# One level of Strassen's algorithm for the large products of a decoder layer in split fp32

## The chip, the cores and the metric

The kernel runs on one core of a Trainium2 chip. The metric is the device time of one execution in microseconds (us). In the profile PE is TensorE (PEld its weight loads), DVE is VectorE, ACT is ScalarE, POOL is GpSimd and SP the engine that issues the transfers; PEclk is the granted TensorE clock as a share of full speed.

## The reference

One decoder layer for 1,024 tokens of 1,024 channels, all in fp32:

```python
def _swiglu(xn, w_gate, w_up, w_down):
    return (jax.nn.silu(xn @ w_gate) * (xn @ w_up)) @ w_down
...
    u = jax.nn.gelu(z[..., :i1])
    v = jax.nn.gelu(z[..., i1:i2])
    c = z[..., i2:i3]
    ga = z[..., i3:i4]
    gb = z[..., i4:]
    a = _spatial_gating(u, v, sgu_norm_g, sgu_w, sgu_b)
    b = _pool_mixer(c, pool_w, pool_scale)
    y = jax.nn.sigmoid(ga) * (a @ w_out_a) + jax.nn.sigmoid(gb) * (b @ w_out_b)
    return y @ w_o
...
        f = _swiglu(_rmsnorm(h, ffn1_pre_g[i]), ffn1_w_gate[i], ffn1_w_up[i], ffn1_w_down[i])
        h = h + 0.5 * _rmsnorm(f, ffn1_post_g[i])
        m = _token_mixer(_rmsnorm(h, mix_pre_g[i]), w_in[i], sgu_norm_g[i], sgu_w[i], sgu_b[i],
                         pool_w[i], pool_scale[i], w_out_a[i], w_out_b[i], w_o[i])
        h = h + _rmsnorm(m, mix_post_g[i])
        f = _swiglu(_rmsnorm(h, ffn2_pre_g[i]), ffn2_w_gate[i], ffn2_w_up[i], ffn2_w_down[i])
        h = h + 0.5 * _rmsnorm(f, ffn2_post_g[i])
        gate = jax.nn.sigmoid(_rmsnorm(h, ple_pre_g[i]) @ ple_w_gate[i])
        e = p[i] @ ple_w_proj[i]
        h = h + _rmsnorm(gate * e, ple_post_g[i])
```

Here `z = xn @ w_in` has 5 x 1,024 columns; the feed-forward layers are 2,816 wide. The spatial gating multiplies each chunk of 128 positions by four masked 128 x 128 matrices; the pool mixer takes trailing means and one 256 x 256 product per group of channels. There are two feed-forward layers, before and after the mixer, with weights of their own.

## The kernel before

Every fp32 product is made of three TensorE products of fp32r parts: an operand is split into hi (a cast on ScalarE) and lo (the operand less hi, on VectorE), and `mm3` adds lo x hi, hi x lo and hi x hi into one PSUM bank of 128 x 512 (lines 134 to 136). The activations stand transposed in SBUF as two halves of 512 tokens, hi and lo, for a whole stage.

The weights come through one ring for the whole program, the class `Weights`: it lists all weight tiles (512 KB each, 128 x 1,024 elements) in the order of their use, loads two ahead, splits them (cast on line 67, subtraction on line 68) and holds four split tiles. A tile is split as soon as a place in the ring is free, whatever stage it belongs to.

A feed-forward layer (`ffn`) goes through 11 groups of 256 hidden channels. For a group it makes gate and up products (`gate_up`: 512 tokens a bank, Silu on ScalarE, multiplication and split), and with a lag of one group the down product of these channels for all eight token tiles (`down`), which VectorE adds into SBUF (line 383). The hidden activations never leave SBUF. With the last group's down product each token tile is closed: post-norm, residual, pre-norm of the next stage (lines 420, 421, 157; the squares on ScalarE, line 147, the reciprocal root on GpSimd, lines 141 and 142), and, LAG = 3 tiles later, its transposes (line 180) and the first products of the next stage (`follow`) are put between the down products.

The mixer then makes v and u by tokens, c with the pooled channels, the gates, the branches a and b and the output projection, each with the weights of the ring; the layer ends with the second feed-forward layer and the gate with the embedding p.

The order of each engine's instructions comes from a scheduler of the framework, which works from the order in the code and the dependences. Each engine runs its instructions in order. All transfers are issued by SP, in order as well.

## Time and profile before

| | |
|---|---|
| time, median of 3 runs | 2355.18 us (2353.83 to 2357.21) |
| span of the profiled execution (its time from the first to the last instruction) | 2353.6 us |
| mean granted TensorE clock | 0.998 |
| matmuls of 128x512 / of 128x256 / of 128x128 and transposes | 9,984 / 96 / the rest of 10,420 |
| bytes moved, mean rate | 179.60 MB, 76 GB/s |
| weight splits of 128x1024: cast, subtraction | 202 x 1,054 ns, 202 x 1,222 ns |
| additions of the down products into SBUF | 320 x 686 ns |

A group's row reads: line, engine, operation, output <- inputs, shape, count, busy time and the mean of one. Matmuls overlap, so that the mean of one (389 ns) is longer than the time from one to the next. A timeline row reads: start, duration, engine, line, operation, and in brackets the idle time before it and what ended it.

### The profile page before, as it was taken

The page shows a single profiled execution, that of the slowest core. Times are in us where ns is not written, and L with a number is a line of the kernel's source. Part 1 is how long each engine was busy: PE and PEld are TensorE (multiplying, and loading weights), DVE is VectorE, ACT ScalarE, POOL GpSimd, SP SyncE. Part 2 cuts the span into 40 slices and gives each one's busy share as a digit, 9 for nine tenths or more (in the row PEclk, how much of TensorE's full clock was granted, in tenths as well). Part 3 has the DMA queues.
Part 4 walks back from the last instruction along what each step waited for, and adds up shares of the span by engine and source line. Part 5 has one row for each costly group of instructions (what it writes and reads, how often), then busy time and mean ns, then how long its engine had stood idle before and what let it go on. Part 6 is the DMA issues. An engine that isn't in the chain of part 4 may idle for free.

```text
span 2353.6 us, 24731 instructions
## 1 busy us (share of the span) xinstructions
PE 2324.4 (99%) x10420; PEld 1925.2 (82%) x10420; DVE 928.5 (39%) x1164; ACT 556.6 (24%) x837; POOL 111.2 (5%) x200
## 2 busy tenths in 40 slices
PE   8999999999999999999999999999999999999998
PEld 6888888888887888888888888788888888888877
DVE  5233333333336652353112253633333333333574
ACT  6211111111112423232221121421111111111252
POOL 1000000000001220000000000200000000000051
PEclk9999999999999999999999999999999999999999
DMA  8111111111112321124233341521111111111323
GB/s 277 53 39 52 54 36 54 54 46 45 54 58 90 126 63 36 49 89 136 90 97 95 123 142 41 176 92 54 44 46 54 54 45 45 54 45 45 98 95 103
DMA packets 179695, 179.60 MB, mean 76 GB/s; under 512 B 7936, under 2 KB 141568, under 8 KB 179584
## 3 DMA queue, kind: packets, MB, share of 16 engines
q1 hardware_dynamic: 179584, 178.03, 23.8%
q8 instruction: 81, 1.33, 0.2%
q14 instruction: 30, 0.25, 0.0%
HBM read 148.64 MB, written 29.36 MB: 76 GB/s over the span
## 4 chain that ended last, share of the span: by engine, by line
PE 64%; DVE 1%; POOL 1%; ACT 1%; issue 0%; DMA 0%; POOLq 0%; DVEq 0%; ACTq 0%
PE ps L134 21%; PE ps L135 21%; PE ps L136 21%; PE ps L180 1%; ACT wk L147 0%; DVE X L421 0%; POOL sc L142 0%; POOL sc L141 0%; DVE wk L157 0%; DMA raw<-in_ffn_w_gate_dram 0%; POOL X L668 0%; POOL part L153 0%; DVE wlo L68 0%; DVE X L420 0%; DVE X L130 0%
## 5 line engine op out<-in xcount | busy, mean ns | idle before, releaser
L135 PE MATMUL ps<-X,whi 128*128 128x512 f32 x2080 | 807.4, 389 | 0.0
L136 PE MATMUL ps<-X,whi 128*128 128x512 f32 x2080 | 807.3, 389 | 0.0
L134 PE MATMUL ps<-X,wlo 128*128 128x512 f32 x2080 | 802.1, 390 | 0.2 <-ACT X L129 0.2
L134 PE MATMUL ps<-whi,X 128*128 128x512 f32 x1184 | 462.1, 392 | 5.0 <-DVE X L130 5.0
L135 PE MATMUL ps<-wlo,X 128*128 128x512 f32 x1184 | 461.7, 390 | 0.0
L136 PE MATMUL ps<-whi,X 128*128 128x512 f32 x1184 | 461.6, 390 | 0.0
L134 PEld LDWEIGHTS ps<-X,wlo 128*128 128x128 f32 x2080 | 390.3, 188 | 81.3 <-ACT X L129 0.7
L136 PEld LDWEIGHTS ps<-X,whi 128*128 128x128 f32 x2080 | 390.5, 188 | 81.1
L135 PEld LDWEIGHTS ps<-X,whi 128*128 128x128 f32 x2080 | 390.5, 188 | 80.5
L67 ACT CAST whi<-raw 128x1024 fp32r<-128x1024 f32 (+1 forms) x206 | 213.4, 1046 | 915.1 <-PE ps L134 518.6
L68 DVE TENSOR_TENSOR wlo<-raw,whi 128x1024 fp32r<-128x1024 f32 (+1 forms) x206 | 247.9, 1212 | 410.8 <-ACT whi L67 386.5
L383 DVE TENSOR_TENSOR X<-X,ps 128x512 f32<-128x512 f32 x320 | 218.7, 686 | 160.9 <-PE ps L136 160.9
L134 PEld LDWEIGHTS ps<-whi,X 128*128 128x128 f32 x1184 | 223.0, 188 | 51.3 <-DVE X L130 5.9
L136 PEld LDWEIGHTS ps<-whi,X 128*128 128x128 f32 x1184 | 223.0, 188 | 46.5
L135 PEld LDWEIGHTS ps<-wlo,X 128*128 128x128 f32 x1184 | 223.1, 188 | 45.3
L362 DVE TENSOR_TENSOR hf<-hf,ps 128x512 f32<-128x512 f32 x88 | 60.5, 688 | 500.4 <-PE ps L136 492.6
L129 ACT CAST X<-hf 128x512 fp32r<-128x512 f32 x88 | 54.6, 621 | 241.3 <-DVE hf L362 241.3
L361 ACT ACTIVATE hf<-ps 128x512 f32<-128x512 f32 x88 | 52.4, 595 | 169.1 <-PE ps L136 169.1
L130 DVE TENSOR_TENSOR X<-hf,X 128x512 fp32r<-128x512 f32 x88 | 60.6, 688 | 28.8 <-ACT X L129 28.8
L130 DVE TENSOR_TENSOR X<-ps,X 128x512 fp32r<-128x512 f32 x85 | 55.1, 683 | 19.2 <-ACT X L129 18.8
L141 POOL TENSOR_SCALAR sc<-sc 128x1 f32<-128x1 f32 x48 | 19.2, 400 | 828.6 <-ACT wk L147 827.5
L147 ACT ACTIVATE wk<-X 128x1024 f32<-128x1024 f32 (+1 forms) x48 | 47.4, 989 | 41.4 <-DVE X L421 32.4
(95 smaller groups left out, 875.0 us busy)
## 6 DMA issues: line engine op xcount, KB each, us to landing
raw<-in_ffn_w_gate_dram SPq DMA_DIRECT2D x44, 512.0 KB, 3.7
raw<-in_ffn_w_up_dram SPq DMA_DIRECT2D x44, 512.0 KB, 3.7
raw<-in_ffn_w_down_dram SPq DMA_DIRECT2D x44, 512.0 KB, 3.7
raw<-in_w_in_dram SPq DMA_DIRECT2D x40, 512.0 KB, 3.7
ld<-h SPq DMA_DIRECT2D x16, 512.0 KB, 3.6
X<-in_x_dram SPq DMA_DIRECT2D x8, 512.0 KB, 10.3
ld<-in_x_dram SPq DMA_DIRECT2D x8, 512.0 KB, 4.3
e<-hf SPq DMA_DIRECT2D x16, 256.0 KB, 4.0
```

What stands on the lines that cost most here:

```text
L67: nc.scalar.copy(hi, raw)
L68: nc.vector.tensor_tensor(lo, raw, hi.bitcast(F32), op=ALU.subtract)
L129: nc.scalar.copy(hi, src)
L130: nc.vector.tensor_tensor(lo, src, hi.bitcast(F32), op=ALU.subtract)
L134: nc.tensor.matmul(ps, wl[1], wr[0], start=first, stop=False)
L135: nc.tensor.matmul(ps, wl[0], wr[1], start=False, stop=False)
L136: nc.tensor.matmul(ps, wl[0], wr[0], start=False, stop=last)
L147: nc.scalar.activation(junk, src, AF.Square, accum_out=ss)
L180: nc.tensor.transpose(ps[:, j * P:(j + 1) * P], src[:, c * P:(c + 1) * P], ident)
L361: nc.scalar.activation(s, pg, AF.Silu)
L362: nc.vector.tensor_tensor(s, s, pu, op=ALU.mult)
L383: nc.vector.tensor_tensor(f[:, cols], f[:, cols], ps, op=ALU.add)
```

## The change

Every large product is cut into 2 x 2 blocks of its three matrices, and seven block products, of sums of blocks, stand in place of eight (Winograd's form: 7 products; 4 sums of the left blocks, 4 of the right, 7 of the results). The blocks of a product's left side are 512 x 512 for the mixer's products. The three-part split is as before, of each of the seven operands. The class `Weights` and the function `ffn` are gone; each stage has pools of its own, which are opened when the stage begins and closed when it ends.

The order of the seven products and the PSUM banks: two banks X and Y for each output block's set of four; a product with `True` begins its bank, the others add to it, so that part of the result sums is made in PSUM.

```diff
+ORDER = (("p1", "X", True), ("p2", "Y", True), ("p5", "Y", True), ("p6", "X", False),
+         ("p3", "Y", False), ("p7", "X", False), ("p4", "X", False))
...
+        def sums(self, k, cols, a11, a12, a21, a22, tmp):
+            s1, s2, s4 = tmp(), tmp(), tmp()
+            nc.vector.tensor_tensor(s1, a22, a21, op=ALU.subtract)
+            self.put(2, k, cols, s1)
+            self.put(6, k, cols, a22)
+            nc.vector.scalar_tensor_tensor(s2, a11, -1.0, s1, op0=ALU.mult, op1=ALU.subtract)
+            self.put(3, k, cols, s2)
+            nc.vector.tensor_tensor(a21, a11, a21, op=ALU.subtract)
+            self.put(5, k, cols, a21)
+            nc.vector.scalar_tensor_tensor(s4, a12, -1.0, s2, op0=ALU.mult, op1=ALU.subtract)
+            self.put(4, k, cols, s4)
...
+        def read(self, name):
+            x, y, at = self.b.get("X"), self.b.get("Y"), self.place
+            if name == "p1":
+                nc.scalar.copy(at("11"), x)
+            elif name == "p2":
+                nc.vector.tensor_tensor(at("11"), at("11"), y, op=ALU.add)
+                self.final("11", at("11"))
+            elif name == "p5":
+                nc.scalar.activation(at("22"), y, AF.Copy, scale=-1.0)
+            elif name == "p6":
+                nc.scalar.activation(at("12"), x, AF.Copy, scale=-1.0)
+            elif name == "p3":
+                nc.vector.tensor_tensor(at("12"), at("12"), y, op=ALU.subtract)
+                self.final("12", at("12"))
+            elif name == "p7":
+                nc.vector.tensor_tensor(at("22"), at("22"), x, op=ALU.subtract)
+                self.final("22", at("22"))
+            else:
+                self.final("21", x)
```

`put` splits one operand into hi and lo. The left operands of a stage are seven tiles of a pool of seven. `feed` makes them out of a token tile by eight transposes: for the upper four tiles it keeps the blocks and makes operands 0 and 1, for the lower four it makes the sums above.

`columns` makes products with weights as the stationary side, for a group of 256 weight columns of each half at a time: `prepare(g)` loads the four blocks, makes 4 additions and 7 splits of 128 x 1,024, and is called for the next group after this group's third product. It serves the hidden stage (11 groups), u and c, the gates (4 groups each) and the branches (2 groups each). `rows` does the same with tokens as the stationary side, for v, the output projection and the last gate.

A feed-forward layer is two stages now. The first writes the seven sums of the hidden activations and four of the down weights' sums into DRAM, per group; the second (`ffn_down`) loads both operands of each of the seven products again, splits them and accumulates over the 11 blocks in PSUM:

```diff
+            def after(c):
+                g = hid.pop(c)
...
+                keep(0, g["11"])
+                keep(1, g["12"])
+                keep(6, g["22"])
+                s1, s2, s3, s4 = (new() for _ in range(4))
+                nc.vector.tensor_tensor(s1, g["22"], g["21"], op=ALU.subtract)
+                keep(2, s1)
...
+                down_sums(c)
...
+            l = s_d[s][i][:, c * HT:(c + n) * HT].rearrange("p (k f) -> p k f", k=n)
+            for j, d in enumerate((l, right(i, c, n))):
+                ld = q.tile([P, 2, HT], F32, name="land", tag="land", bufs=4)[:, 0:n]
+                nc.sync.dma_start(ld, d)
+                split(o[:, j, 0, 0:n], o[:, j, 1, 0:n], ld)
...
+        def final(t, half, part):
+            ft = tiles[t]
+            if t >= 4 and half == 0:
+                nc.scalar.copy(ft[:, half * HT:(half + 1) * HT], part)
+            if half != (1 if t < 4 else 0):
+                return
+            hp = load(q, src(t), lds)
+            xn = work(q, wks)
+            r = rsqrt(squares(ft, xn), factor / D, factor * EPS)
+            nc.vector.tensor_tensor(ft, ft, g_post, op=ALU.mult)
+            nc.vector.scalar_tensor_tensor(ft, ft, r, hp, op0=ALU.mult, op1=ALU.add)
+            nc.sync.dma_start(dst[t], ft)
+            pre_norm(ft, g_pre, xn)
+            left.feed(xn, t)
```

`final` is the closing of a token tile (`closing`): the upper four tiles are complete with p3, the lower four with p4, the last product. There is no lag: a tile's transposes follow its norms at once. The large products done so are gate, up and down, the five of `w_in`, both branches, the output projection and the last gate; the pooled channels' products and the projection of p are as they were. The spatial products have v as the stationary side now and 128 columns each, with the bias in an addition on VectorE; the results u, c, a and y go through DRAM between the stages.

**TensorE at a stage end.** In the first feed-forward layer's down stage, before, the transposes of a token tile (line 180, `wk` is the normed tile) stand between down products whose operands have been there for long (`whi`, `wlo`: activations and weights split before):

```order
L134 MATMUL ps_4818<-whi_4540,X_4301 128x512
L135 MATMUL ps_4818<-wlo_4541,X_4301 128x512
L136 MATMUL ps_4818<-whi_4540,X_4301 128x512
L180 MATMUL ps_4826<-ident_135,wk_4721 128x128 x4
L180 MATMUL ps_4833<-ident_135,wk_4721 128x128 x4
L134 MATMUL ps_4859<-whi_4534,X_4301 128x512
```

Now the first token tile's transposes (line 167) stand right between the end of p3 (`X_4549`, which completes this tile) and the start of p7 (`X_4720`):

```order
L86 MATMUL ps_4003<-X_4549 128x512
L87 MATMUL ps_4003<-X_4549 128x512
L88 MATMUL ps_4003<-X_4549 128x512
L167 MATMUL ps_4590<-ident_117,wk_4573 128x128 [waits DVE_49]
L167 MATMUL ps_4590<-ident_117,wk_4573 128x128 x3
L167 MATMUL ps_4595<-ident_117,wk_4573 128x128 x4
L86 MATMUL ps_3612<-X_4720 128x512 [waits DVE_49,Activation_49]
```

The transposes moved from three tiles after the end of their tile's products to the place directly behind them.

**VectorE at the same stage's end.** Before, the splits of the next weights (line 68) stand among the closings of the last tiles (lines 420, 421 and 157; line 130 splits transposed tiles):

```order
L157 SCALAR_TENSOR_TENSOR wk_4990<-X_1144,sc_5003,g_4697 128x1024
L68 TENSOR_TENSOR wlo_5101<-raw_4687,whi_5100 128x1024
L420 TENSOR_TENSOR X_1144<-X_1144,g_4695 128x1024
L68 TENSOR_TENSOR wlo_5107<-raw_4693,whi_5106 128x1024
L130 TENSOR_TENSOR X_4702<-ps_5138,X_4701 128x4x128
L421 SCALAR_TENSOR_TENSOR X_1144<-X_1144,sc_5069,ld_5007 128x1024
```

Now the last token tile's sums (lines 149 to 156) and operand splits (line 82, `X`) come first, and the first split of the next stage's weights (`wr_5321`, for v) stands behind all of them:

```order
L149 TENSOR_TENSOR hf_5280<-ps_5273,hf_5278 128x512
L152 SCALAR_TENSOR_TENSOR hf_5281<-f_4713,hf_5280 128x512
L154 TENSOR_TENSOR hf_5278<-f_4713,hf_5278 128x512
L82 TENSOR_TENSOR X_5105<-hf_5280,X_5105 128x4x128
L156 SCALAR_TENSOR_TENSOR hf_5282<-f_4713,hf_5281 128x512
L82 TENSOR_TENSOR X_5108<-ps_5273,X_5108 128x4x128
L82 TENSOR_TENSOR X_5112<-hf_5281,X_5112 128x4x128
L82 TENSOR_TENSOR X_5116<-hf_5278,X_5116 128x4x128
L82 TENSOR_TENSOR X_5120<-hf_5282,X_5120 128x4x128
L82 TENSOR_TENSOR wr_5321<-land_5317,wr_5321 128x1024
L82 TENSOR_TENSOR wr_5324<-land_5319,wr_5324 128x1024
```

The weights' splits moved from among the closings to behind the last of them.

**SP between the two stages of a feed-forward layer.** There was no such place before. Now the loads of the down stage (line 441, `land`) stand behind the stores of the last group's sums (lines 403 and 397; `so` are sums made by VectorE):

```order
L403 DMA ffn1_s4_128<-so_3572 128x512
L397 DMA ffn1_t20_138<-so_3584 128x512
L397 DMA ffn1_t30_139<-so_3587 128x512
L397 DMA ffn1_t50_140<-so_3590 128x512
L397 DMA ffn1_t60_141<-so_3593 128x512
L113 DMA g_3608<-in_ffn1_post_g_dram 128x1024
L113 DMA g_3610<-in_mix_pre_g_dram 128x1024
L441 DMA land_3617<-ffn1_s0_124 128x1024
L441 DMA land_3621<-in_ffn1_w_down_dram 128x2x512
L441 DMA land_3650<-ffn1_s0_124 128x1024
```

What is new in this queue are all the stores and the two gains ahead of the first load.

More of the change, by code (lines that the diff above doesn't have):

```diff
@@ L1 @@
-from contextlib import ExitStack
+from contextlib import ExitStack, contextmanager
 import concourse.bass as bass
@@ L343, in layer_kernel @@
[L343 to L373 removed]
+    ws_t = const.tile([P, 2, SGU_G, P], FR, name="ws_t")
@@ new lines, in down_stage, with new @@
+    def down_stage(s, src, dst, next_g):
+        with stage(f"{s}b") as q:
+            def new():
+                return q.tile([P, D], F32, name="f", tag="f", bufs=9)
+            f = [new() for _ in range(NT)]
+            g_post, g_pre = gain(q, a[f"{s}_post_g"][0]), gain(q, next_g)
+            nxt = Seven(q, new)
+            ffn_down(s, q, closing(q, f, 4.0, src, dst, g_post, g_pre, nxt))
+        return nxt
+    ffn_hidden("ffn1", left)
+    left = down_stage("ffn1", lambda t: x[t * P:(t + 1) * P, :], h1_d, a["mix_pre_g"][0])
@@ new lines, in layer_kernel, with new @@
+    with stage("o") as q:
+        def new():
+            return q.tile([P, D], F32, name="m", tag="m", bufs=9)
+        m = [new() for _ in range(NT)]
+        g_post, g_pre = gain(q, a["mix_post_g"][0]), gain(q, a["ffn2_pre_g"][0])
+        left = Seven(q, new)
+        rows(q, ysum, a["w_o"][0], closing(q, m, 1.0, lambda t: h1_d[t], h2_d, g_post, g_pre, left, 1, 2), lands=6, wts=2)
+    ffn_hidden("ffn2", left)
+    h3_d = scratch("h3_", NT)
+    left = down_stage("ffn2", lambda t: h2_d[t], h3_d, a["ple_pre_g"][0])
```

1020 lines of the change are left out of this document (515 added, 505 removed).

## The prediction, as put on record before the change was run

> **What bounds the kernel now.** I read the page first (totals, then the chain that ended last), then the groups with shapes kept apart, then busy time by window, then the timeline of single engines at a stage end.
>
> ```profile
> span 2353.6 us, 24731 instructions
> PE 2324.4 (99%) x10420; PEld 1925.2 (82%) x10420; DVE 928.5 (39%) x1164; ACT 556.6 (24%) x837; POOL 111.2 (5%) x200
> PE 64%; DVE 1%; POOL 1%; ACT 1%; issue 0%; DMA 0%; POOLq 0%; DVEq 0%; ACTq 0%
> ```
>
> TensorE is busy for 99% of the span and is the only engine with a real share of the chain (what the chain line lacks to 100% is its short pieces). VectorE has 61% idle, ScalarE 76%. So each matmul taken out is worth its full step, as long as TensorE stays the bound. The step is not the mean duration, since matmuls overlap; it comes from a window that holds nothing but feed-forward work:
>
> ```profile
> core 0: us, PE busy (x) PEld busy (x) DVE busy (x) ACT busy (x) POOL busy (x), PEclk, DMA share, GB/s
> 0.00:60.00 60.00, 49.96 (x232) 40.90 (x233) 31.19 (x36) 36.38 (x62) 7.86 (x39) 0.97 0.80 272
> 1600.00:2100.00 500.00, 500.00 (x2208) 414.15 (x2207) 180.33 (x234) 82.69 (x106) 0.00 (x0) 1.00 0.16 49
> ```
>
> 500.00 / 2208 = **0.2265 us** for a 128x512 matmul. The span is 1.6 us below the median of the runs, 2355.18; I sum in the span and add 1.6 at the end.
>
> **What goes.** The order of the instructions holds 8,760 matmuls of 512 columns after the change, where there were 9,984: 1,224 x 0.2265 = 277 us less. It is not a full eighth, since the pooled channels and the small projection of p stay as they are. The 96 spatial matmuls of 256 columns become 192 of 128, and 276 transposes stay (272 before): 468 short ones. A group of eight transposes shows their step:
>
> ```profile
> 765.78 1.03 PE L180 MATMUL ps<-ident,wk 128*128 128x128 f32 x8
> 766.57 0.48 PE L134 MATMUL ps<-whi,X 128*128 128x512 f32 x1
> ```
>
> 0.79 / 8 is 0.10; with the gap to the next matmul 0.11. No row has an fp32r matmul of 128 columns; 0.06 (a quarter of the 512 step) and 0.23 (the whole of it) bound it, 12 to 43 us for the 192; I take the transpose's 0.11. TensorE's work is then 8,760 x 0.2265 + 468 x 0.11 = 1984 + 51 = **2035 us**. If nothing else made it wait beyond what it does today, the span would be about 2,085 (today's waits are 2353.6 less 9,984 x 0.2265, less 42 of short matmuls: 50 us).
>
> **What comes.** Every operand is a sum that has to be made and split. In the order, VectorE's subtractions and additions of 128x1024 go from 240 to 616, those of 128x512 between SBUF tiles from 164 to 506, its PSUM additions fall from 533 to 363; ScalarE's casts of 128x1024 go from 222 to 430; the loads and stores on SP go from 398 to 1,102, their bytes from 180 to about 367 MB. Steps, from start to start at a stage end:
>
> ```profile
> 767.73 1.28 DVE L157 SCALAR_TENSOR_TENSOR wk<-X,sc,g 128x1024 f32<-128x1024 f32 x1 [2.19 <-POOL sc L142]
> 768.93 1.22 DVE L420 TENSOR_TENSOR X<-X,g 128x1024 f32<-128x1024 f32 x1
> 770.06 0.69 DVE L458 BATCH_NORM_STATS2 st<-X 128x6 f32<-128x512 f32 x1
> ...
> 771.85 0.68 DVE L383 TENSOR_TENSOR X<-X,ps 128x512 f32<-128x512 f32 x1
> 772.45 1.28 DVE L421 SCALAR_TENSOR_TENSOR X<-X,sc,ld 128x1024 f32<-128x1024 f32 x1
> ```
>
> ```profile
> 789.53 1.06 ACT L147 ACTIVATE wk<-X 128x1024 f32<-128x1024 f32 x1 [0.15 <-DVE X L421]
> 790.50 0.18 ACT L147 ACTIVATION_READ_ACCUMULATOR wk<-X 128x1 f32 x1
> 790.59 1.03 ACT L67 CAST whi<-raw 128x1024 fp32r<-128x1024 f32 x1
> 791.52 1.06 ACT L147 ACTIVATE wk<-X 128x1024 f32<-128x1024 f32 x1
> ```
>
> VectorE: 1.13 us for 1024 columns of two tiles, 1.20 with a scalar, 0.60 for 512. ScalarE: 0.93 for a cast, 1.06 for squares. VectorE's sum over the program is then about 1,500 us, ScalarE's 980: both below TensorE's 2,035. So the average says that all is hidden. By stage it is not, and the queues are in order, so I go through the stages (TensorE / VectorE in us, from counts and steps): prologue 31 / 42; hidden of each feed-forward 419 / 258; down 216 / 150; v 97 / 77; u and c 152 / 74; gates 174 / 105; **branches a and b 152 / 174**; **output projection 83 / 87**; last gate 76 / 62. Two stages are VectorE's. Inside hidden, u and c, and the first four products of down, each wait of TensorE is for work that VectorE's order has several us earlier, so I cost those at nothing; their cover is VectorE's idle 40%, and 419 us for the 66 MB of hidden's loads and stores (158 GB/s, less than the 272 of the first row above). Were the cover gone, each microsecond per group would be 22 in the 22 groups.
>
> **Where TensorE waits.** These are the terms; each is a chain that stands between two matmuls in the order.
>
> - *Start.* 14 us until inputs have landed and gone through the first norm, then the prologue's 42 us of VectorE, all ahead of the first weight's split, and some 5 us for hand-offs: 61 where TensorE has 31 to do. **+30** (21 to 41).
> - *Hidden to down, twice.* The first loads stand on SP behind the last group's stores, which wait for VectorE's sums. Nine steps of 0.60, two issues, a landing, two casts, a subtraction:
>
> ```profile
> raw<-in_ffn_w_down_dram SPq DMA_DIRECT2D x44, 512.0 KB, 3.7
> X<-in_x_dram SPq DMA_DIRECT2D x8, 512.0 KB, 10.3
> ```
>
> ```profile
> 783.13 0.33 SPq L423 DMA_DIRECT2D h<-X  x1
> 783.50 0.42 SPq L166 DMA_DIRECT2D ld<-in_x_dram  x1
> ```
>
> 5.4 + 0.8 + 3.7 + 2 x 0.93 + 1.13 + hand-offs of 1 = 14. (The 10.3 is a landing in the burst at the start, for later.) What follows is slow as well:
>
> ```profile
> 769.16 0.39 PE L136 MATMUL ps<-whi,X 128*128 128x512 f32 x1
> 771.39 0.50 PE L134 MATMUL ps<-X 128*128 128x512 f32 x1 [1.84 <-DVE X L130]
> ...
> 773.09 0.63 PE L136 MATMUL ps<-X 128*128 128x512 f32 x1
> 773.51 0.63 PE L134 MATMUL ps<-X 128*128 128x512 f32 x1
> 773.94 0.63 PE L135 MATMUL ps<-X 128*128 128x512 f32 x1
> ```
>
> ```profile
> 770.00:780.00 10.00, 8.61 (x35) 7.05 (x36) 7.23 (x11) 4.09 (x9) 2.19 (x5) 0.83 0.32 106
> ```
>
> After 1.84 us of idleness the granted clock of that window is 0.83, and matmuls come every 0.43 us for about 3 us: 1.6 to 2 us lost behind each long wait. [...] So 14 + 2, twice: **+32** (26 to 40).
> - *Inside down, twice.* The first token tile's eight transposes stand ahead of the seventh factor's matmuls. They wait for its closing: addition 0.6, squares 1.06, multiply 1.13 with POOL beside it, an addition of the next tile 0.6, 1.20, squares 1.06, POOL, 1.20; and then ScalarE's two copies and two casts of the transposed tile (0.5 each) stand ahead of p7's own two casts of 0.93. POOL's pair is one of two lengths:
>
> ```profile
> 766.86 0.19 POOL L141 TENSOR_SCALAR sc<-sc 128x1 f32<-128x1 f32 x1 [2.72 <-ACT wk L147]
> 767.14 0.55 POOL L142 TENSOR_TENSOR sc<-sc,nhalf 128x1 f32<-128x1 f32 x1
> 767.90 1.16 POOL L141 TENSOR_SCALAR sc<-sc 128x1 f32<-128x1 f32 x1 [0.21 <-ACT wk L147]
> 769.14 1.41 POOL L142 TENSOR_TENSOR sc<-sc,nhalf 128x1 f32<-128x1 f32 x1
> ```
>
> 0.83 or 2.65 us. With the short one and hand-offs of 1 that is 8.7 to the transposes, of which TensorE works 2 on the other tiles; then 3.9 of ScalarE's. 10 or 11, and 2 for the clock: **+24** for both stages (12 to 36).
> - *Down to the next stage, twice.* p4 ends all four lower token tiles; each has 1.13 + 1.20 + 1.20 of norms and 4 sums and 5 subtractions of 512, 9 us, and all stand on VectorE ahead of the next weights' split. From the end of the first tile's last matmul: 10 us to its transposes, 31 of queue, 1.2 of split, 2 of gaps; less 6 of matmuls and 3 of transposes. 35 + 2, twice: **+74** (64 to 90). Before, the lag of three tiles hid this.
> - *v to u and c* **+22** (18 to 30): VectorE runs late by 7 at the end of v, then store, load, split. *To the gates* **+11** (8 to 16). *Pooled channels*, four groups, each with a split behind the next group's: **+17** (8 to 26).
> - *Branches and output projection.* VectorE starts 6.5 us late behind stores and loads, has 181 us to the last of the sums, and the output projection's first weights another 10: 198 against TensorE's 152, and 4 for the clock: **+50** (38 to 75).
> - *Output projection to the second feed-forward.* VectorE has 67 us left when p3 ends, 50 into the 83: 117 less 83, hand-offs 6, clock 2: **+42** (35 to 52).
> - *Tail.* Four tiles of 3.1 us on VectorE behind p4, and the store: **+15** (8 to 22).
> - *Hand-offs.* The chains above are mostly laid end to end. VectorE's gaps of 2.19 us behind POOL's long pair, quoted above, will recur: **+15** (0 to 50).
>
> 2035 + 30 + 32 + 24 + 74 + 22 + 11 + 17 + 50 + 42 + 15 + 15 = **2367 us** of span, 2369 as a median. What is saved on TensorE, 277, is a little less than what the stage ends give back.
>
> **Rivals.**
> *The chains overlap better.* With most terms near their lower ends (they sum to 238, so 2273 at the least) the span is 2290 to 2350. For it: several chains are counted whole where some of it may run ahead. Against: each sits on an in-order queue.
> *Seven eighths.* All stalls hide, as the average suggests: 2,085. Against it are the 31 us of VectorE's queue at three stage ends.
> *Landings starve the down product; this one ends slower.* Each 512 KB tile has 2.72 us of matmuls, and four tiles are in the ring. A tile's round is its landing and about 3 us of issue, cast and subtraction, so it is hidden while a landing takes under 4 x 2.72 - 3 = 7.9 us. The rows above show 3.7 us at the usual rates and 10.3 in the burst of 272 GB/s; down asks for 230. At 10.3 a tile takes 13.3 / 4 = 3.3 us: 0.6 over 77 tiles is 46 us, twice 92: 2460.
> *The clock stays down.* In branches a and b TensorE waits often for VectorE. If each wait is followed by the slow matmuls of the row above, the 672 there cost up to 0.2 more, 135 us; the waits themselves swallow about 30: 2470. [...]
> That the change saves no matmuls is ruled out by the count in the order.
>
> **How the numbers follow.** Forecast 0.48, better overlap 0.26, seven eighths 0.04, starved landings 0.14, slow clock 0.08. About 0.2% is what a measurement of this kernel can tell from no change: 2350.5 to 2359.9. Faster: 0.26 and 0.04, less 0.02 that falls within, and 0.04 of the forecast's lower end: 0.32. Same: 0.02 and 0.10 of the forecast: 0.12. Slower: the rest, 0.56. The range goes from the better overlap's lower end, 2295, to the starved landings, 2455; the forecast's own is 2330 to 2410.
>
> **What would show it.** Right: about 9,230 matmuls and 2,035 us of TensorE steps; VectorE near 65% busy; a dozen stretches in which TensorE is idle for over 5 us, the longest (35 to 45) after each down and after the output projection with VectorE as the releaser, and PEclk below 1 behind each; windows inside hidden with TensorE full. Wrong: idle time spread within hidden or down, released by DMA (starved landings); matmuls of 0.63 us all through branches a and b (clock); stage ends under 20 us (better overlap). The sum's weakest terms are the queue behind down, taken twice, and the hand-offs.

## The result, and the profile after

The changed kernel takes **2410.32 us** (median of 4 runs, 2403.43 to 2414.13) against 2354.72 for the kernel before in the same runs: a ratio of **1.0231** (95% interval 1.0214 to 1.0247), 56 us slower. The prediction was 2369, 14 us slower: the direction is right and the time lies in its range, but the size is wrong by 41 us.

The page of the changed kernel: totals, the granted clock in 40 slices of the span, and the chain that ended last:

```profile
span 2412.3 us, 25287 instructions
PE 2114.9 (88%) x9228; PEld 1740.2 (72%) x9228; DVE 1495.2 (62%) x1811; ACT 951.3 (39%) x1349; POOL 109.3 (5%) x176
PEclk9899999989986979999998997969999998998888
PE 51%; issue 30%; DVE 8%; DMA 6%; ACT 3%; POOL 1%; SPq 1%; DVEq 0%; ACTq 0%; POOLq 0%
```

The clock row of the kernel before:

```profile
PEclk9999999999999999999999999999999999999999
```

The counts are as forecast: 1,192 matmuls fewer, VectorE at 1,495 us. TensorE is busy for 88% instead of 99%, and the clock row, all nines before, dips at the start and at each stage end. In the chain, "issue" is time in which an engine waited for nothing that the profile shows. Busy time by windows, the columns as in the prediction's (PEclk is the third number from the end):

```profile
1700.00:1800.00 100.00, 100.00 (x443) 82.78 (x442) 61.48 (x71) 33.48 (x44) 0.00 (x0) 1.00 0.46 153
740.00:783.00 43.00, 12.07 (x48) 9.46 (x47) 37.91 (x50) 24.38 (x43) 10.99 (x14) 0.57 0.46 159
871.00:906.00 35.00, 19.36 (x88) 17.77 (x87) 18.99 (x45) 5.85 (x7) 3.09 (x3) 0.56 0.69 188
1556.00:1609.00 53.00, 15.58 (x64) 12.46 (x63) 49.20 (x61) 31.56 (x58) 16.38 (x21) 0.55 0.56 173
```

Inside a hidden stage (first row) nothing is lost. Behind the down product (740) and the output projection (1556) VectorE is busy for about 90% of the window while TensorE is busy for 12 to 16 us. Between v and u/c (871) more than TensorE's waits is lost, since the clock is 0.56 there.

I split the span by the matmul records: work is 8,760 full steps of 0.2265 us and 468 short ones of 0.109; idle is the sum of TensorE's gaps, with the 4.9 us ahead of its first matmul; "slow clock" is the busy time within stretches at half clock less the full-speed time of the matmuls that start in them; the tail is what follows the last matmul.

| us | before | forecast | after |
|---|---|---|---|
| TensorE's work at full steps | 2308.9 | 2035 | 2035.2 |
| idle, hand-offs | 21.3 | 299 | 272.1 |
| slow clock | 3.2 | 18 as itemised | **62.0**, in 20 stretches |
| tail | 7.9 | 15 | **25.3** |
| rest (what is left; 6 us of it lie in the first 74 us) | 12.3 | - | 17.8 |
| span | 2353.6 | 2367 | 2412.3 |

So the saving came as counted, and the waits came out nearly right in sum; the slow clock was not, and then the tail. (The first expectation below speaks of 22 us priced for the clock; the items of the sum add to 18.) These are the questions for the runs.

### The profile page after: what moved, and what is told of

Same layout as the page of the kernel before. It is cut to its first block, busy times and chain, and to the rows that moved or that the text cites. A ratio compares the mean times of both kernels' runs of the same rounds, so it can differ in the third digit from the quotient of the medians.

```text
span 2412.3 us, 25287 instructions
## 1 busy us (share of the span) xinstructions
PE 2114.9 (88%) x9228; PEld 1740.2 (72%) x9228; DVE 1495.2 (62%) x1811; ACT 951.3 (39%) x1349; POOL 109.3 (5%) x176
## 4 chain that ended last, share of the span: by engine, by line
PE 51%; issue 30%; DVE 8%; DMA 6%; ACT 3%; POOL 1%; SPq 1%; DVEq 0%; ACTq 0%; POOLq 0%
PE ps L86 17%; PE ps L87 17%; PE ps L88 17%; DVE X L82 2%; ACT X L81 1%; DMA out_dram<-ld 1%; ACT wk L99 1%; POOL sc L94 1%; SPq L237 1%; POOL sc L93 1%; DMA lb<-b 1%; DVE wt L82 1%; DVE wk L109 1%; DVE hf L152 1%; DVE hf L149 0%
## 5 line engine op out<-in xcount | busy, mean ns | idle before, releaser
L86 PE MATMUL ps<-X,wt 128*128 128x512 f32 x1904 | 745.8, 394 | 60.9 <-DVE wt L82 49.8
L87 PE MATMUL ps<-X,wt 128*128 128x512 f32 x1904 | 747.9, 393 | 2.5 <-DVE X L82 2.5
L88 PE MATMUL ps<-X,wt 128*128 128x512 f32 x1904 | 743.0, 392 | 0.0
L86 PEld LDWEIGHTS ps<-X,wt 128*128 128x128 f32 x1904 | 360.7, 190 | 141.8 <-DVE wt L82 51.7
L87 PEld LDWEIGHTS ps<-X,wt 128*128 128x128 f32 x1904 | 362.0, 190 | 79.9 <-DVE X L82 4.8
L88 PEld LDWEIGHTS ps<-X,wt 128*128 128x128 f32 x1904 | 361.6, 190 | 75.8
L86 PE MATMUL ps<-X 128*128 128x512 f32 x616 | 239.9, 397 | 40.6 <-ACT X L81 33.5
L82 DVE TENSOR_TENSOR X<-land,X 128x1024 fp32r<-128x1024 f32 x168 | 186.2, 1134 | 134.2 <-ACT X L81 132.4
L87 PE MATMUL ps<-X 128*128 128x512 f32 x616 | 243.2, 395 | 0.0
L88 PE MATMUL ps<-X 128*128 128x512 f32 x616 | 242.8, 394 | 0.0
L81 ACT CAST X<-land 128x1024 fp32r<-128x1024 f32 x168 | 160.5, 983 | 185.4 <-PE ps L88 84.0
L81 ACT CAST wt<-raw 128x1024 fp32r<-128x1024 f32 x136 | 142.7, 1050 | 198.3 <-PE ps L88 115.3
L82 DVE TENSOR_TENSOR wt<-tsum,wt 128x1024 fp32r<-128x1024 f32 x102 | 124.7, 1223 | 114.9 <-ACT wt L81 114.8
L82 DVE TENSOR_TENSOR wt<-raw,wt 128x1024 fp32r<-128x1024 f32 x136 | 166.3, 1223 | 45.8 <-ACT wt L81 45.6
L86 PEld LDWEIGHTS ps<-X 128*128 128x128 f32 x616 | 117.5, 191 | 66.6 <-ACT X L81 42.2
L86 PE MATMUL ps<-wr,X 128*128 128x512 f32 x336 | 128.7, 403 | 30.2 <-ACT wr L81 30.2
L87 PEld LDWEIGHTS ps<-X 128*128 128x128 f32 x616 | 117.9, 191 | 25.0
L88 PEld LDWEIGHTS ps<-X 128*128 128x128 f32 x616 | 117.8, 191 | 24.7
L87 PE MATMUL ps<-wr,X 128*128 128x512 f32 x336 | 132.9, 396 | 0.0
L88 PE MATMUL ps<-wr,X 128*128 128x512 f32 x336 | 131.7, 394 | 0.0
```

The costliest lines, as they stand in the source:

```text
L81: nc.scalar.copy(hi, src)
L82: nc.vector.tensor_tensor(lo, src, hi.bitcast(F32), op=ALU.subtract)
L86: nc.tensor.matmul(ps, wl[1], wr[0], start=first, stop=False, skip_group_check=True)
L87: nc.tensor.matmul(ps, wl[0], wr[1], start=False, stop=False, skip_group_check=True)
L88: nc.tensor.matmul(ps, wl[0], wr[0], start=False, stop=last, skip_group_check=True)
```

## The experiments

Each is an edit of the changed kernel. A delta is against its 2410.3 us, a ratio against the kernel before, which ran beside every group of runs (medians of 2355.3 to 2355.9). The changed kernel's own four runs spread over 10.7 us, so a delta is good to some 5 us, and gains of 11 to 16 us are not to be ranked by size.

**The clock: fill the waits.** Matmuls of the spatial weights into an unused bank, 706 in all (the expectation says 690), are put behind the last matmul ahead of each long wait:

```diff
+    def warm(n, after=None):
+        ps = bank()
+        with tc.issue_after((after or last_mm[0]).ins):
+            for _ in range(n):
+                nc.tensor.matmul(ps, ws_t[:, 0, 0, :], ws_t[:, 0].rearrange("p g s -> p (g s)"), ...)
```

> The changed kernel with 690 idle matmuls (their result is read by nobody) put into TensorE's order at its long waits, sized somewhat shorter than each wait, so that the array is busy while it waits. Nothing else moves. Theory clock (the half-rate stretches behind the waits are what I priced at 22 us and the records show as 62): they go except those of the start, and the time falls by 40 to 55 us, to about 2360. Rival A (the slow matmuls lie beside VectorE's queue, which sets the end of those stages anyway): the clock reads near 1.0 and the time falls by less than 15 us. Rival B (the fillers delay what follows them): slower than the changed kernel.

Measured: 2395.41 us, minus 15, ratio 1.0175 (1.016 to 1.019): a good part less than the theory's 40 to 55. The slow clock fell from 62 to 37 us, not to nothing. By the same split the fillers (706 x 0.2265 = 160 us) and the idle time left (113) come to 273 us, where 272 were idle before, so the waits end about where they ended; the profiled execution is 19 us shorter, the 25 of clock less 6 of rest. TensorE's timeline between hidden and down shows why; of the changed kernel first:

```profile
512.64 2.08 PE L86 MATMUL ps<-X 128*128 128x512 f32 x4 [16.66 <-ACT X L81]
514.52 0.63 PE L87 MATMUL ps<-X 128*128 128x512 f32 x1
```

and with the filling (line numbers are shifted):

```profile
504.70 3.79 PE L90 MATMUL ps<-ws_t 128*128 128x512 f32 x16
511.52 2.05 PE L97 MATMUL ps<-X 128*128 128x512 f32 x4 [3.04 <-ACT X L81]
513.37 0.63 PE L98 MATMUL ps<-X 128*128 128x512 f32 x1
...
517.21 0.63 PE L98 MATMUL ps<-X 128*128 128x512 f32 x1
```

A wait of 16.66 us was filled up to a remainder of 3.04, and the matmuls behind it still take 0.63 us, in place of the 0.39 that most of the changed kernel's take, for over 4 us. What is left of this wait costs as much clock as the whole of it (2.8 us, where the whole cost 2.0). That asks for the price by length and by distance.

**The clock: its price measured.** In the second hidden stage, where TensorE never waits, a chain of small ScalarE copies between two matmuls makes 36 waits (`ch`):

```diff
+    def hold(n):
+        ps = bank()
+        with tc.issue_after(last_mm[0].ins):
+            nc.tensor.transpose(ps[:, 0:P], ident, ident)
+        nc.scalar.copy(chain[0], ps[:, 0:P])
+        for i in range(n):
+            nc.scalar.copy(chain[(i + 1) % 2], chain[i % 2])
+        held[0] = nc.tensor.transpose(ps[:, P:2 * P], chain[n % 2], ident)
```

In the changed kernel's trace the shortest of the 20 stretches at half clock, five of them, last 3.413 us each, the others 6.8 to 47.8.

> The price of the clock, measured by itself: in the hidden stage of the second feed-forward, where TensorE has no wait in the changed kernel, waits are put in by a chain of small ScalarE copies between two matmuls: three single ones (some 2, 5 and 10 us), five of about 2 us with 24 matmuls (5.4 us) between them, ten with 12 matmuls (2.7 us) between them, eighteen with 3 or 6 matmuls (0.7 or 1.4 us) between them. Theory (each wait, long or short, opens a stretch of about 3.4 us at half clock, and waits that recur keep it open): lost to the clock some 2 us for each single wait, 1.7 for each of the five, 1.3 to 1.7 for each of the ten, about 0.9 for each of the eighteen: some 45 us in all for the 36 waits. Rival (the prediction's rule taken by length, 2 us behind a wait of over 5 us and nothing behind shorter ones): 4 us. Rival (2 us behind every wait, however close): 72.

Measured, from the trace of a single run (2568 us in all, with some 100 us of waits put in). TensorE's timeline, in which a row with 168, 24, 12 or 3 matmuls is what stands behind one wait:

```profile
1653.17 0.33 PE L94 MATMUL ps<-ident,ch 128*128 128x128 f32 x1 [2.34 <-ACT ch L93]
1653.25 38.36 PE L101 MATMUL ps<-X,wt 128*128 128x512 f32 x168
...
1753.16 0.48 PE L94 MATMUL ps<-ident,ch 128*128 128x128 f32 x1 [13.54 <-ACT ch L93]
1753.29 40.78 PE L101 MATMUL ps<-X,wt 128*128 128x512 f32 x168
```

```profile
1898.83 0.48 PE L94 MATMUL ps<-ident,ch 128*128 128x128 f32 x1 [2.39 <-ACT ch L93]
1898.96 4.32 PE L101 MATMUL ps<-X,wt 128*128 128x512 f32 x12
...
1905.77 0.33 PE L94 MATMUL ps<-ident,ch 128*128 128x128 f32 x1 [2.39 <-ACT ch L93]
1905.85 3.02 PE L101 MATMUL ps<-X,wt 128*128 128x512 f32 x12
...
2026.52 0.47 PE L94 MATMUL ps<-ident,ch 128*128 128x128 f32 x1 [2.39 <-ACT ch L93]
2026.65 1.63 PE L101 MATMUL ps<-X,wt 128*128 128x512 f32 x3
```

A wait of 13.54 us makes the 168 matmuls behind it 2.42 us longer than a short one that costs nothing; one of 6.95 cost 2.31. Of sixteen waits of 2.33 to 2.39 us, eleven cost 1.25 to 1.6 us each (4.32 for twelve matmuls) and five nothing (3.02). The eighteen close ones cost 18.6 together, about 1.0 each, with nearly all of their matmuls at half speed. The sum is 40 us for 36 waits, where the theory had 45 and its rivals 4 and 72. So in this run the price is per wait and grows little with the length: for about 2.35 us it is nothing or some 1.5, on the mean 1.0, and for 7 and 13.5 us it is 2.3 and 2.4. Where it begins was not measured; the wait of 1.84 us in the prediction's row had it. The changed kernel has **38 waits of over 2 us**, counting the one ahead of its first matmul.

**Inside down: two pairs of the seventh factor first.** `operands` and matmuls of p7's first two pairs are written ahead of p3's readout:

```diff
+            if i == 4:
+                for kp in range(2):
+                    run(5, kp)
             rest = [operands(i, kp) for kp in range(outer, pairs)]
```

> The changed kernel with two thirds of nothing removed: in the down stage the matmuls of the first two pairs of p7 (48 matmuls, 10.9 us) are written ahead of the closings of the first four token tiles. Theory (the first tile's transposes and the casts behind them stand in TensorE's and ScalarE's queue between p3 and p7): the waits of 6.8 and 3.6 us in each down stage go, with 3 us of slow clock each, together 24 to 28 us; about 2384. Rival (VectorE is the bound of p7 and p4, so that the wait comes back later in p7 or at the stage's end): less than 10 us.

Measured: 2394.66 us, minus 16, ratio 1.0165 (1.015 to 1.018): between theory and rival. TensorE's waits there, before and after the edit:

```profile
671.29 1.97 PE L167 MATMUL ps<-ident,wk 128*128 128x128 f32 x8 [6.78 <-DVE wk L109]
676.85 2.04 PE L86 MATMUL ps<-X 128*128 128x512 f32 x4 [3.58 <-DVE X L82]
```

```profile
676.86 1.09 PE L167 MATMUL ps<-ident,wk 128*128 128x128 f32 x8 [1.29 <-DVE wk L109]
681.61 2.04 PE L86 MATMUL ps<-X 128*128 128x512 f32 x4 [3.66 <-DVE X L82]
```

The first wait is covered, the second is not: the transposed tile's copies and casts still stand ahead of the third pair's. That was the second half of the prediction's chain at this place, and it is a wait of its own.

**Hidden to down: operands loaded earlier.** The first two pairs of down's operands are loaded and split ahead of the last group's sums, in the hidden stage's raw tiles:

```diff
+            if early and g == groups - 1:
+                early()
             after(g)
```

> The changed kernel with the first two operand pairs of the down product loaded and split in the hidden stage's own tiles, ahead of the last group's sums and stores. Theory (SP's order puts the loads behind the last group's stores): the waits of 16.7 and 16.8 us between hidden and down go, with 2 to 3 us of clock each: 33 to 39 us less, about 2374. Rival (the operand tiles come free only when the last group's products end, or VectorE's sums stand ahead of the split): under 12 us.

Measured: 2395.85 us, minus 14.5, ratio 1.0175 (1.016 to 1.019): little more than the rival's 12. The wait of 16.66 us became one of 9.09, now behind the two early pairs:

```profile
505.81 0.39 PE L88 MATMUL ps<-X 128*128 128x512 f32 x1
515.29 1.22 PE L86 MATMUL ps<-X 128*128 128x512 f32 x2 [9.09 <-ACT X L81]
```

The third pair's loads (`land`) still stand on SP behind the last group's stores:

```profile
501.90 3.07 SPq L415 DMA_DIRECT2D ffn_t<-so  x4
506.02 0.42 SPq L461 DMA_DIRECT2D land<-ffn_s  x1
```

Not quite half is gained; the wait is where it was predicted, in SP's order.

**All stores from GpSimd's queue.** Each `nc.sync.dma_start` that stores becomes `nc.gpsimd.dma_start`, but for those of the token tiles' closings and of the output.

> The changed kernel with the stores of e, of the sums in the hidden stage, and of v, u, c, the gates and the branches issued by GpSimd in place of SP, so that no load stands behind a store. Theory (in-order SP is a part of the waits at the start, hidden to down, v to u and c, u and c to the gates): 15 to 45 us less. Rival (those waits are the chain of landing, cast and split itself, or GpSimd issues its transfers so slowly that VectorE's reciprocal roots wait): no change or slower.

Measured: 2387.36 us, minus 23, ratio 1.0132 (1.0116 to 1.0149). The wait at hidden to down falls from 16.7 to 12.4 and 11.9 us, that ahead of the gates from 9.8 to 2.9, that ahead of the branches from 15.1 to 10.4. The two between v and u/c grow, from 4.4 and 11.2 to 7.3 and 12.1. In this run GpSimd's stores of v's results start about 3.0 us apart there, and VectorE waits six times, 11.9 us in all, for the tiles that they free; two of the stores, and one of the waits:

```profile
874.20 0.88 DVE L618 TENSOR_TENSOR hf<-ps,sb 128x128 f32<-128x128 f32 x4 [1.96 <-DMA sv_d<-hf]
874.41 0.78 POOL L619 DMA_DIRECT2D sv_d<-hf  x1 [1.67 <-issue]
877.49 0.82 POOL L619 DMA_DIRECT2D sv_d<-hf  x1 [0.52 <-issue]
```

So the theory holds on the whole, and in one stage a part of the rival (slow issuing by GpSimd) does.

**Down to the next stage: the next product first.** v's (and the last gate's) first product needs only the upper token tiles. It is made ahead of the lower tiles' closings, in four PSUM banks of its own:

```diff
+            ow = next_weights() if i == 6 else None
...
+        banks = next_product(ow)
+        for t in range(4):
+            outs[t].read("p4")
+        return banks
```

> The next stage's first product (48 matmuls of 512 columns, 10.9 us; it needs only the upper four token tiles) is made ahead of the closings of the lower four, with its two weight tiles loaded and split there, at both stage ends behind a down product. Theory (VectorE's queue of 9.06 us for each lower token tile, in front of the next weights' splits, sets when the next stage begins): TensorE does 10.9 us of work inside each of the two waits and has that much less to do behind them; idle time falls from 272 us by about 22, the time by 18 to 26, to about 2388. Rival (the chain of the first lower tile's closing, or the PSUM banks that the product holds, sets the end): the waits move back by what was put in, and the time falls by less than 8.

Measured: 2397.99 us, minus 12, ratio 1.0186 (1.0171 to 1.0201): between the two. From the end of the last down product to VectorE's last operand, of the changed kernel and of the edit:

```profile
741.70:777.50 35.80, 6.90 (x33) 5.57 (x32) 33.97 (x46) 20.05 (x39) 10.99 (x14) 0.55 0.39 129
```

```profile
741.00:782.10 41.10, 16.41 (x81) 13.29 (x79) 34.13 (x46) 22.09 (x44) 11.99 (x14) 0.71 0.48 174
```

VectorE has the same 34 us of work in both, and in the changed kernel 1.8 of idleness: its queue is the bound, as predicted. In the edit the 48 matmuls lie inside the window, but it is 5.3 us longer, nearly all of it idleness of VectorE:

```profile
751.50 1.28 DVE L520 SCALAR_TENSOR_TENSOR f<-f,sc,ld 128x1024 f32<-128x1024 f32 x1 [0.44 <-POOL sc L94]
754.53 0.69 DVE L149 TENSOR_TENSOR hf<-ps,hf 128x512 f32<-128x512 f32 x1 [1.75 <-ACT hf L183]
```

The first tile's sums (line 149), at 746.97 in the changed kernel, start at 754.53, since its transposes now stand on TensorE behind the product made ahead. The long block of matmuls in front of transposes that feed the bound gave about half of its gain back here; put between the transposes, it might not. That was not tried.

**The two ends.** The spatial weights get a tile of their own, loaded ahead of the token loop; the last four residuals and embeddings are loaded together:

```diff
-        ws = half_tile(q).rearrange("p (g s) -> p g s", g=SGU_G)
+        ws = q.tile([P, HT], F32, name="ws", tag="ws", bufs=1).rearrange("p (g s) -> p g s", g=SGU_G)
...
+            if t == 4 and half == 0:
+                for u in range(4, NT):
+                    es[u] = load_e(u, 0)
+                    held[u] = q.tile([P, 2, HT], F32, name="land", tag="land", bufs=7).rearrange("p k f -> p (k f)")
+                    nc.sync.dma_start(held[u], h3_d[u])
```

> Two ends of the program: the spatial weights get a tile of their own and are loaded ahead of the token loop (the wait of 13.67 us at 53.7 us was for them, behind the stores on SP); and for the last gate's lower four tiles the residuals and embeddings are loaded together ahead of the four closings, not each behind the store of the tile before. Theory (SP's order makes both): the 13.67 us wait goes, and the first hidden product, now at 74, starts at 67 to 70, when VectorE is through with its 42 us; the time behind the last matmul falls from 25.3 us to 15 to 17; together minus 12 to 16. Rival (VectorE and ScalarE set both ends, SP only follows): minus 0 to 5.

Measured: 2398.8 us, minus 11.5, ratio 1.0181 (1.0166 to 1.0196). The tail on VectorE, of the changed kernel (`ld` is the residual, loaded from `h`):

```profile
2397.15 1.29 DVE L841 TENSOR_TENSOR ld<-ld,m 128x512 f32<-128x512 f32 x2 [1.58 <-DMA ld<-h]
...
2402.58 1.29 DVE L841 TENSOR_TENSOR ld<-ld,m 128x512 f32<-128x512 f32 x2 [2.82 <-DMA ld<-h]
2408.02 1.29 DVE L841 TENSOR_TENSOR ld<-ld,m 128x512 f32<-128x512 f32 x2 [4.15 <-DMA ld<-h]
```

Each addition waits for a residual: 8.55 us in three waits. What the residuals' loads (line 118) waited for on SP in the last 25 us (in total, times, longest):

```profile
SPq L118 <- DMA out_dram<-ld: 9.8, 3, 4.5
```

There are two tiles `ld` for the residuals, and the sum is stored out of them, so that a load starts only when an earlier output store has landed: the one at 2398.36 starts 0.05 us after the store issued at 2393.84 has. It is thus the reuse of two tiles, more than SP's order, that makes these waits. The edit gives the four residuals tiles of their own as well as an earlier place, and does not tell the two apart. With it VectorE has none of these three waits, and the tail is 16.0 us, the prediction's 15. At the start it is alike: SP was through with the stores at 60.8, and the load of the spatial weights waited until 63.8 for a tile that, by the trace, VectorE was still reading. With the edit the wait for them went, but the first hidden product starts only at 71.1 in place of 74.0: it then waits for VectorE's split of its weights.

**Pooled operands early.** They depend on nothing in the gates' stage, so they are made at a group's start:

```diff
+            if before:
+                before(g)
             nxt = None
```

> In the gates' stage each group's pooled operands and their weights are made on VectorE at the group's beginning, not at its end behind the next group's splits; the pooled products stay where they are. Theory (the four waits in front of the pooled products, 4.3, 4.3, 4.3 and 2.6 us, with the 2.5 us behind one of them and 9.9 us of slow clock, come from VectorE's order alone): all of them go, minus 20 to 28. Rival (VectorE's or the transfers' work in this stage is what lasts, and TensorE then waits at the next group's first product): minus 0 to 10.

Measured: 2380.52 us, **minus 30**, ratio 1.0107 (1.0091 to 1.0122), the theory's upper end and beyond. One of the four places, in the changed kernel:

```profile
1105.87 1.04 ACT L81 CAST wt<-tsum 128x1024 fp32r<-128x1024 f32 x1 [2.10 <-PE ps L88]
...
1109.35 0.68 DVE L82 TENSOR_TENSOR pw<-hd,pw 128x512 fp32r<-128x512 f32 x1
1110.09 0.50 PE L86 MATMUL ps<-df,pw 128*128 128x512 f32 x1 [4.30 <-DVE pw L82]
...
1111.35 0.63 PE L87 MATMUL ps<-df,pw 128*128 128x512 f32 x1
```

A cast of the next group's operands stands ahead of `pw` on ScalarE, and their subtraction and a sum on VectorE, and the 0.63, 0.39 at full clock, shows the clock's price on top of the 4.30. In windows that hold the same 768 matmuls of the stage, the changed kernel and then the edit:

```profile
1065.00:1275.00 210.00, 187.80 (x768) 152.42 (x768) 112.44 (x130) 81.88 (x112) 0.00 (x0) 0.93 0.36 117
```

```profile
1062.00:1245.00 183.00, 176.79 (x768) 145.59 (x768) 112.72 (x131) 80.47 (x112) 0.00 (x0) 0.98 0.43 138
```

Idle time falls by 16 us, and busy time by 11 without one matmul less; 9.9 of these are the slow clock of that stage by the split above.

**Sums on GpSimd.** Three of the four sums of a left operand go to GpSimd:

```diff
-            nc.vector.scalar_tensor_tensor(s2, a11, -1.0, s1, op0=ALU.mult, op1=ALU.subtract)
+            nc.gpsimd.tensor_tensor(s2, a11, s1, op=ALU.add)
...
+            nc.gpsimd.tensor_tensor(a21, a11, a21, op=ALU.subtract)
+            nc.gpsimd.tensor_tensor(s4, s2, a12, op=ALU.subtract)
```

> Three of the four sums of each left operand (512 columns, between tiles in SBUF) go from VectorE to GpSimd, which is 95% idle: in the prologue 4 sets, at the three stage ends 4 each, in the branches 12. Theory (VectorE's queue sets those ends, and GpSimd takes the sums at about the 0.64 us of its one row of 512 columns): VectorE has 1.8 us less for each set, 7 at the start, 7 at each stage end, 22 in the branches: 50 in all, of which 30 to 45 show in the time. Rival (a sum takes GpSimd much longer than VectorE's 0.60, or the two hinder each other; the casts and subtractions of the sums then come later, and GpSimd's reciprocal roots stand behind them): no gain, up to 20 slower.

Measured: 2448.71 us, **plus 38**, ratio 1.0398 (1.0381 to 1.0415). The rival holds, with more than the 20 us it allowed for. VectorE at a stage end with GpSimd beside it, and a group of GpSimd's:

```profile
756.07 0.68 DVE L82 TENSOR_TENSOR X<-ps,X 128x512 fp32r<-128x512 f32 x1
756.67 1.15 DVE L156 SCALAR_TENSOR_TENSOR X<-hf,X 128x512 fp32r<-128x512 f32 x1
757.95 1.80 DVE L82 TENSOR_TENSOR X<-hf,X 128x512 fp32r<-128x512 f32 x1
757.94 1.26 POOL L159 TENSOR_TENSOR hf<-hf,f 128x512 f32<-128x512 f32 x1
```

```profile
L152 POOL TENSOR_TENSOR hf<-lb,hf 128x512 f32<-128x512 f32 x10 | 26.5, 2646 | 521.5 <-DMA raw<-in_w_out_a_dram 399.4 <-ACT X L81 58.7 <-ACT hd L216 39.5
```

A sum takes GpSimd 1.3 to 2.6 us, where VectorE has 0.60 (the row of 0.64 us that the theory went by is an operation with one input), and VectorE's own subtraction of 512 columns takes up to 1.80 in place of 0.68 beside it. How much of the 38 us each of the two makes was not told apart. An idle engine was no spare engine.

**Together.** First p7's pairs, down's early pairs (three of each), the stores, the two ends and the product ahead:

> All together: three pairs of the sixth product ahead of the closings inside down, three pairs of down's operands ahead of the last group's sums, all stores but the final ones issued by GpSimd, the two ends, and the next stage's first product ahead of the lower closings. If the waits are places of their own, the gains of the single runs add, less some 8 us between the hidden stage and down where two of them remove the same wait: 16 + 15 + 23 + 14 + 22 - 8 = 82 less than the 2410 of the change, 2328, faster than the kernel before by 1.1%. If they share one bound (VectorE's queue or the transfers), what one removes comes back at the next place: 2350 to 2375.

Measured: 2337.22 us (2332.84 to 2341.26), ratio **0.9916** (0.990 to 0.9933): 73 us of the 82, nearer to waits that are places of their own. The five gains measured one by one (16, 14.5, 23, 11.5 and 12) less the 8 for the place that two of them share make 69. With the pooled operands made early and the GpSimd sums:

> The combination before (2337) with the pooled operands made early and the three sums on GpSimd, the branches' stores back on SP. If both gains hold and add: minus 20 to 28 and minus 20 to 40: 2270 to 2300. If GpSimd hinders, as in the rival of the run before, the pooled part alone remains: 2310 to 2320.

Measured: 2345.25 us, ratio 0.9958 (0.9943 to 0.9973): outside both ranges: GpSimd takes back more than the pooled part gives. And without those sums:

> The first combination (2337) and the pooled operands made early, nothing else. The pooled waits lie in a stage that none of the combination's other parts touches but for the stores, so the 30 us of the single run should come off whole: 2302 to 2312, faster than the kernel before by about 2%. If the stores on GpSimd had already taken a part of these waits, 2312 to 2325.

Measured: **2315.01 us** (2310.68 to 2315.84), ratio **0.9821** (0.9808 to 0.9835): 22 of the 30 us came off. The stores on GpSimd had taken little of the pooled waits (18.0 us in the changed kernel, 16.6 in the first combination); but the wait ahead of the gates' first product, 2.9 us in the first combination, is 6.13 here, since the first group's pooled work now stands there and VectorE waits with it for c's store:

```profile
1032.61 0.07 DVE L753 MEMSET pc<- 128x16 f32 x1 [4.91 <-DMA c<-hd]
```

This version beats both kernels. Its page:

```profile
span 2314.1 us, 25499 instructions
PE 2093.6 (90%) x9228; PEld 1725.7 (75%) x9228; DVE 1493.9 (65%) x1811; ACT 948.4 (41%) x1349; POOL 324.1 (14%) x554
```

By the same split as above it has 202.8 us idle, 41.0 of slow clock and a tail of 17.8.

## Why the prediction came out as it did

- **The saving** (277 us and the short matmuls): right. The work is 2035.2 us where 2035 was forecast. The spatial matmuls of 128 columns, bounded by 0.06 and 0.23, have a step of 0.111 at full clock; 0.11 was taken. (The kernel before has 340 transposes, not 272; the sum does not use them.)
- **Inside hidden, u and c, and the first products of down nothing waits**: right. TensorE has no gap there, and the landings that would have starved down took 4.7 to 4.9 us (medians), far from 7.9. That rival fell. (Its 230 GB/s for down should be 193 by its own 512 KB in 2.72 us; the trace has 194 over 140 us of the stage.)
- **The waits at the stage ends**: right in place. Forecast and measured, with the clock's loss behind each:

| us | forecast: idle, clock | measured: idle, clock |
|---|---|---|
| start | 30, 0 | 34.7, 5.1 |
| hidden to down, twice | 28, 4 | 33.5, 5.0 |
| inside down, twice | 20, 4 | 20.7, 6.2 |
| down to the next stage, twice | 70, 4 | 59.0, 10.0 |
| v to u and c | 22, 0 | 15.6, 8.2 |
| to the gates | 11, 0 | 9.8, 2.2 |
| pooled channels | 17, 0 | 18.0, 9.9 |
| branches | 46, 4 | 43.3, 8.6 |
| output projection to the second feed-forward | 40, 2 | 37.4, 6.8 |
| hand-offs | 15, 0 | - |
| sum | 299, 18 | 272, 62 |

That several lines agree so well in sum (74 and 69, 22 and 24, 42 and 44) is partly luck: idle time counted too high stands for clock left out. Causes were tested by moving one thing each: SP's order (early operands, stores), the closing ahead of p7, VectorE's order at the pooled channels. For down to the next stage, the branches and the output projection VectorE's queue is read from the trace; the run with the product ahead bears on the first, and gave back in time about half of the work that it put into the waits.
- **The clock: this step failed.** "1.6 to 2 us lost behind each long wait" was about right for a long wait, but the sum charges it to nine waits and puts it at nothing for all others, though the row that it was read from is a wait of only 1.84 us. In the changed kernel's trace half clock stands within 3.5 us behind 36 of the 38 waits of over 2 us, long or short (the other two lie ahead of the first record of the clock, at 18.6 us): 62 us in place of 18. And the chain behind a down product, taken as one wait of 35 us, is five waits of 2.6 to 7.9, with a tile's transposes between them:

```profile
751.53 1.94 PE L167 MATMUL ps<-ident,wk 128*128 128x128 f32 x8 [6.13 <-DVE wk L109]
760.59 1.94 PE L167 MATMUL ps<-ident,wk 128*128 128x128 f32 x8 [7.12 <-DVE wk L109]
```

Behind the output projection there are six such waits. So the sign "a dozen stretches of over 5 us, the longest 35 to 45" did not come: there are 24, the longest 17.2. That the clock's loss is time lost is shown in part by the filling (25 us of it off, 15 to 19 of time), and at one place by the pooled operands.
- **The pooled term** (17, measured 27.9) is the same mistake in one place: 18.0 us idle, nearly as forecast, 9.9 of clock left out.
- **The tail** (15, measured 25.3): VectorE's part was right, but the residuals' loads, which wait for output stores to land, were put at nothing. The run on the ends brought it to 16.0.
- **The start**: the first hidden product was forecast at 61 and starts at 74.0. The spatial weights' load, behind the prologue's stores on SP and then waiting for a tile, made part of it; without it 71.1 remain, 10 more than forecast. Which piece of the prologue was taken too short, no run told apart.
- **The other rivals**: the clock did not stay down in branches a and b (52 us lost there, where that rival had some 150), and neither seven eighths nor the better overlap came.
- **Hand-offs** of 15 cannot be found as waits of their own. The 17.8 us of rest have no term in the sum, though the kernel before has 12.3 by the same split; what they are, no run shows.

In sum: idle time 27 less than forecast, clock 44 more, tail 10 more, rest 18: 45 us of span.

## What to carry to other kernels

Fewer matmuls pay only as far as the stages' ends do: here an eighth less work on TensorE was lost until loads, stores and the next stage's first operands were put in an order that lets TensorE run on, and then it paid 1.8%. Count waits, not only their sum: half clock followed 36 of the 38 of over 2 us here, so that filling most of a wait gained little and removing the pooled channels' short ones gained more than their length (30 us for 18 of idle time). Before work is moved to an idle engine, measure what its neighbour loses.

## What was not expected of the hardware

- **The clock's edges lie on a grid.** In the changed kernel's trace the granted clock is full or one half, and its 41 edges lie within 4 ns of multiples of 3.4133 us from each other. Cut into steps of that length, from the first record of the clock on (at 14.4 and 18.6 us), the traces of the kernel before and of the changed kernel hold 1,282 steps at full clock. The 20 in which TensorE was idle for over 56% were all followed by half clock; of eight with 44 to 56%, four were; of the 1,254 with less, none. Full clock came back 22 times, each time behind a step with at most 10% idle. Where a wait falls on this grid may be why of sixteen equal waits of 2.35 us eleven cost something and five nothing; no run tested it.
- GpSimd's sums of 512 columns took 1.3 to 2.6 us, with VectorE's 0.68 us beside them stretched up to 1.80.
- With the stores on GpSimd, its stores of v's results started about 3.0 us apart, and VectorE waited for the tiles.
